# A small DMA for the norm vector, a later parameter packet, and another matmul order in the first chunk

## The chip, the cores and the metric

The kernel runs on one core of a Trainium2 chip. The time is device microseconds (us) of one execution; shown are three runs of the kernel before and, for the profile, one profiled execution. Engines: PE (TensorE, with PEld for its weight loads), DVE (VectorE), ACT (ScalarE), POOL (GpSimd), SP (SyncE, which issues nearly all DMAs). Matmul operands are fp32r: a float32 value is split into a rounded high half and an exact low half.

## The reference

The reference is a trunk of two layers over x of 1 x 256 x 2048 in float32, with RMSNorm ahead of each layer and at the end. Only the beginning matters here:

```python
h = rmsnorm(x, norm_g)                      # x * rsqrt(mean(x*x) + eps) * norm_g
proj = h @ w_in                             # 2048 -> 5120
xa, ga, zb, gb = split(proj)                # zb = (u, v)
ya = s5_mixer(xa, lam_re, lam_im, log_dt, b, c, d)   # constants: exp, cos, sin of lam * dt
...                                         # gates, layernorm of v, spatial gate, w_out, residual
x = x + o @ w_out                           # layer 1: differential attention, rope, w_out
return rmsnorm(x, final_norm)
```

## The kernel before, in words

All weights pass through one stream of chunks, in the order in which they are used: a chunk is 512 rows (four k tiles of 128) by 512 columns, 1 MB. The first eight chunks are the two column blocks of v: chunks 0 to 3 for the first, 4 to 7 for the second. `fetch` (L139) issues a chunk's DMA on SP into a buffer wr; three buffers take turns. Chunks 0 and 1 come in four pieces, 2 and 3 in two, and ahead of each piece comes the piece of x transposed (xt) for the same k tiles. Behind chunk 5 come the two loads of x by tokens (xk), later the other constants.

`split` (L156) makes the halves of a weight: ACT writes wh (rounded), DVE writes wl = w - wh. Both are in half chunks and have three buffers each. `h_split` (L282) does it for the activations, with the norm vector g0 as a scale per partition: ACT writes hh, DVE writes hl. The norm's factor per token is applied to the product later; it comes from `x_norm` (L302): a Square with a running sum on ACT for each xk (scratch tile xsq), then small operations on DVE. `gemm_t` (L201) does three matmuls per k tile and half of the tokens: hh by wh, hh by wl, hl by wh. PE's queue keeps the order of the program, and so do the other engines'.

The parameter packet pkt (L259) holds 164 floats per partition: g0 in columns 0 to 15, then the second norm vector, the parameters of the state space model, biases and others. It is the first DMA. From it `ssm_params` (L359) makes the constants of the state space model with a long run of small DVE operations (`exact_exp`: e_x, e_n, e_r, e_p; then the tiles ph_s, ph_c, pw). `diag_skip` (L452) has POOL write 16 tiles "intra" from it. POOL also fills tiles with zeros (memsets of bbr, cA, cN); cA and cN lie where xk was, so their memsets follow the two xsq.

SP's order is that of the program text. On the other engines a planner sets the order when the kernel is built, with a model of the time of each operation and transfer; work under `high_priority`, as in `split`, `h_split` and `x_norm`, goes ahead of other work that is ready at the same moment. Ten warm-up matmuls on a tile of ones (psw, L269) run before the first weights are there.

Of the kernel before, what the change touches and what calls it, by code (L numbers as in the profile page):

```python
# [10 lines left out]
F32 = mybir.dt.float32  # L11
# [6 lines left out]
T = 256  # L18
# [11 lines left out]
def hybrid_trunk_kernel(ctx: ExitStack, tc: tile.TileContext, xT, xtok, w_in0, w_glu, w_out0,  # L30
# [51 lines left out]
        A.activation(out=o, in_=i, func=f, **kw)  # L82

    def rsqrt_mean(name, ss, n, eps, post=None):
        """(ss / n + eps) ** -0.5: an integer first guess, a cubic step and a Newton step."""
        w = ss.shape[-1]

        def t(nm, dt=F32):
            return sm.tile([128, w], dt, name=nm, tag=f"{nm}{w}", bufs=1)

        def v_y2(y):
            z = t("rq_z")
            if w == 1:
                stt(z, y, v, y, ALU.mult, ALU.mult)
            else:
                mul(z, y, y)
                mul(z, z, v)
            return z

        v = t("rq_v")  # L100
        ts(v, ss, 1.0 / n, ALU.mult, eps, ALU.add)
        g = t("rq_i", I32)
        ts(g, v.bitcast(I32), 1, ALU.logical_shift_right)
        ts(g, g, -1.0, ALU.mult, 1597463007.0, ALU.add)
        y = g.bitcast(F32)
        r = sm.tile([128, w], F32, name=name, tag=name, bufs=2)
        z = v_y2(y)
        u = t("rq_u")
        ts(u, z, 0.375, ALU.mult, -1.25, ALU.add)
        mul(u, u, z)  # L110
        stt(r, u, 1.875, y, ALU.add, ALU.mult)
        z = v_y2(r)
        c = 1.0 if post is None else post
        ts(z, z, -0.5 * c, ALU.mult, 1.5 * c, ALU.add)
        mul(r, r, z)
        return r

    # ---------------------------------------------------------------- weight stream
    stream = []
    L0_IN = {"v": (6, 7), "xa": (0, 1), "u": (4, 5), "gb": (8, 9), "ga": (2, 3)}  # L120
    for part in ("v", "xa", "u", "gb", "ga"):
# [14 lines left out]
    pos = {"f": 0, "s": 0, "i": 0}  # L136
    extra_loads = {}

    def fetch(upto):  # L139
        while pos["f"] <= min(upto, len(stream) - 1):  # L140
            i = pos["f"]
            w, n, k = stream[i]
            t = wp.tile([128, 4, 512], F32, name=f"wr{i}", tag="wr", bufs=3)
            src = w[n, k].rearrange("p (a c) -> p a c", a=4)
            step = (1, 1, 2, 2)[i] if i < 4 else 4
            for a in range(0, 4, step):
                if i < 4:
                    xs = slice(4 * i + a, 4 * i + a + step)
                    SP.dma_start(out=xt[:, xs, :], in_=xT[:, xs, :])
                SP.dma_start(out=t[:, a:a + step], in_=src[:, a:a + step])  # L150
            fetched[i] = t
            for fn in extra_loads.get(i, ()):
                fn()
            pos["f"] += 1

    def split(upto, before=None):  # L156
        """hi = the weight rounded to float32r, lo = the exact rest."""
        while pos["s"] <= min(upto, len(stream) - 1):
            i = pos["s"]
            t = fetched.pop(i)  # L160
            halves[i] = []
            for b in range(2):
                if i >= len(stream) - 4:
                    c = 2 * (i - len(stream) + 4)
                    if b == 0:
                        hb, lb = (t8(LAST[c + z], f"{'hl'[z]}last{i}", [128, 4, 512], F32R) for z in range(2))
                    h, l = hb[:, 2 * b:2 * b + 2], lb[:, 2 * b:2 * b + 2]
                else:
                    h = wp.tile([128, 2, 512], F32R, name=f"wh{i}_{b}", tag="wh", bufs=3)
                    l = wp.tile([128, 2, 512], F32R, name=f"wl{i}_{b}", tag="wl", bufs=3)  # L170
                w = t[:, 2 * b:2 * b + 2]
                with tc.high_priority(offset=AHEAD):
                    step = 1 if i < 2 else 2
                    for a in range(0, 2, step):
                        if before is not None:
                            for z in range(step):
                                before(4 * i + 2 * b + a + z)
                        e = slice(a, a + step)
                        act(h[:, e], w[:, e], AF.Copy)
                        sub(l[:, e], w[:, e], h[:, e].bitcast(F32))  # L180
                halves[i] += [(h[:, a], l[:, a]) for a in range(2)]
            pos["s"] += 1
# [11 lines left out]
    def next_chunk():  # L194
        i = pos["i"]
        pos["i"] += 1
        fetch(i + 3)
        split(i + 1, h_split if i < 3 else None)
        return halves.pop(i)

    def gemm_t(ps, acts, ktiles, first, last):  # L201
        ws = next_chunk()
        for a, k in enumerate(ktiles):
            hi, lo = acts(k)
            wh, wl = ws[a]
            for t in range(2):
                s = slice(t * 128, (t + 1) * 128)
                PE.matmul(ps[:, t, :], hi[:, s], wh, start=first and a == 0, stop=False)  # L208
                PE.matmul(ps[:, t, :], hi[:, s], wl, start=False, stop=False)  # L209
                PE.matmul(ps[:, t, :], lo[:, s], wh, start=False,  # L210
                          stop=last and a == len(ktiles) - 1)

    def gemm_c(ps, acts, ktiles, first, last):
        ws = next_chunk()
# [20 lines left out]
    def side1(name, shape, lane=0):  # L235
        return psb.tile(shape, F32, name=name, tag=f"sb{lane}")

    # ---------------------------------------------------------------- start: x^T, norm
    pkt = const.tile([128, N_PK], F32, name="pkt")
    xt = big.tile([128, 16, T], F32, name="xt", tag="e")  # L240

# [14 lines left out]
    extra_loads[5] = [load_xk]  # L256
    extra_loads[7] = [lambda: SP.dma_start(out=bct, in_=bc)]
    extra_loads[8] = [load_ln]
    SP.dma_start(out=pkt, in_=pk)  # L259
    fetch(8)  # L260
    ident = const.tile([128, 128], F32, name="ident")
    make_identity(nc, ident)
# [4 lines left out]
    psw = side2("psw", [128, 512])  # L267
    for i in range(10):
        PE.matmul(psw[:, 0:128], ones, ones, start=True, stop=True)  # L269
    g0 = pkt[:, 0:16]  # L270
    g1 = pkt[:, 16:32]
    lam_re = pkt[:, 32:64]
    lam_im = pkt[:, 64:96]
# [13 lines left out]

    split(0, h_split)

    # the norm's factor: per token on partitions, and as a row on every partition  # L290
    rbc = const.tile([128, T], F32, name="rbc")
    rsx = {}

# [17 lines left out]
        x_norm()  # L311

    def evac_c(ps, c, name):
        """two of the four channel tiles, times the norm's factor"""
        o = t2(name, [128, 2, T])
        mul(o, ps[:, 2 * c:2 * c + 2, :], rbc.unsqueeze(1).to_broadcast([128, 2, T]))
        return o
# [1 line left out]
    def h_acts(k):  # L319
        return hh[k // 8][:, k % 8, :], hl[k // 8][:, k % 8, :]  # L320

    # ---------------------------------------------------------------- SSM constants
    def p32(name, w=32, dt=F32, bufs=1):
        return sm.tile([128, w], dt, name=name, tag=f"p{w}{name}", bufs=bufs)

# [33 lines left out]
    def ssm_params():  # L359
# [66 lines left out]
        add(fa[:, 1, :], t1, t2_)  # L426
        cst.update(ab=ab, fc=fc, fa=fa, ep=ep)
        yield
        # powers of exp(i * 2 phi): 1, 2, 4, ..., 64
        pw = []  # L430
        prev = ep
        for j in range(7):
# [30 lines left out]
    def ssm_consts():  # L463
# [15 lines left out]
        for key, z_re, z_im, o_re, o_im, sign in (  # L479
# [15 lines left out]
            masked(o_re, m1[:, 0])  # L495
            masked(o_im, m2[:, 0])
            yield
        # K0 = Re(C bb) and the skip, as one matrix per two pairs
        intra = cst["intra"]
        pk0 = side1("pk0", [128, 16, 32])  # L500
        for i in range(16):
# [124 lines left out]
    side.append(e_tables(0))  # L626
    side.append(ssm_consts())

    # ---------------------------------------------------------------- layer 0: v, spatial gate
    G.affine_select(out=bw, in_=bw, pattern=[[0, 8], [1, 128]], compare_op=ALU.is_ge,  # L630
                    fill=0.0, base=0, channel_multiplier=-1)
    vt = t8(13, "vt", [128, 2, 1024])
# [34 lines left out]
    for _ in ssm_bT():  # L667
        pass

    # ---------------------------------------------------------------- layer 0: xa  # L670
    for half in range(2):
        ps = main_c(f"xa{half}")
        for k in range(4):
# [10 lines left out]
        for _ in ssm_half(half):  # L684
            pass

    # ---------------------------------------------------------------- layer 0: u, gb, ga
    ut = t8(8, "ut", [128, 2, 1024])
    for n in range(2):
        ps = main_t(f"u{n}")  # L690
# [44 lines left out]
                gt = evac_c(ps, c, f"at{n}{c}")  # L735
                act(gat[:, n * 4 + 2 * c:n * 4 + 2 * c + 2, :], gt, AF.Silu)

    # ---------------------------------------------------------------- layer 0: output projection
    x1 = [t8(t, f"x1{t}", [128, D]) for t in range(2)]

    def y_acts(k):
# [80 lines left out]
    mul(rope_c, row1, rtab[:, 0])  # L822
    mul(rope_s, row1, rtab[:, 1])

    # ---------------------------------------------------------------- layer 1
    def h2_acts(k):
        return h2h[k // 8][:, k % 8, :], h2l[k // 8][:, k % 8, :]

# [4 lines left out]
    for c in (0, 256):  # L833
        G.affine_select(out=maskt[:, c:c + 128], in_=maskt[:, c:c + 128], pattern=[[-1, 128]],
                        compare_op=ALU.is_ge, fill=NEG, base=0, channel_multiplier=1)
    # lambda
    lprod = const.tile([128, 2], F32, name="lprod")
    lv = lqk.rearrange("p (a b) -> p a b", b=2)
    mul(lprod, lv[:, :, 0], lv[:, :, 1])
# [10 lines left out]
    oh = {}  # L850

    def rope_evac(o, ps, name):
        """o = the rotated, normalised channels; a map's pairs lie on rows 0-15 and 32-47"""
        def row(z, n):
            return z.unsqueeze(1).to_broadcast([n, 4, T])

        m = t4(name, [128, 4, T])
        G.memset(m[0:32], 0.0)
        mul(m[0:16], ps[32:48], row(rope_s[32:48], 16))
        mul(m[32:48], ps[0:16], row(rope_s[0:16], 16))  # L860
        mul(o, ps, row(rope_c, 128))
        add(o[0:48], o[0:48], m[0:48])
# [78 lines left out]
    for p in range(4):  # L941
        qk_hl = []
        for w in range(2):
# [2 lines left out]
                gemm_c(ps, h2_acts, range(k * 4, k * 4 + 4), k == 0, k == 3)  # L946
                run_side(1)
            rope_evac(qkT[:, w], ps, f"rm{p}{w}")
            # the second query block meets all keys: its operands in two exact parts
            src = qkT[:, w, :, 128 * (1 - w):T]  # L950
            hi, lo = (z[:, 512 * w:512 * w + 512 * (1 + w)].rearrange("p (m t) -> p m t", m=4) for z in (qk_hi, qk_lo))
            act(hi, src, AF.Copy)
# [16 lines left out]
        side.append(attention(p, qkT, qk_hl, vh, vl, sg))  # L969
        run_side(1000)  # L970

    # ---------------------------------------------------------------- layer 1: output projection
    def o_acts(k):
        a, b = oh[k // 8]
        return a[:, k % 8, :], b[:, k % 8, :]
# [63 lines left out]
def _layout(i):  # L1039
# [11 lines left out]
    xT = np.ascontiguousarray(x.T.reshape(16, 128, T).transpose(1, 0, 2))  # L1051
    xtok = np.ascontiguousarray(x.reshape(2, 128, D))

    # pairs of groups, ordered (half, qh, ct, q) where the pair is half * 16 + ct * 4 + qh * 2 + q
    order = np.arange(32).reshape(2, 4, 2, 2).transpose(0, 2, 1, 3).reshape(32)

    def state(z):
# [31 lines left out]
    rp[0:16, 0] = rp[32:48, 0] = c  # L1089
    rp[0:16, 1] = z  # L1090
    rp[32:48, 1] = -z
    # rows 16-31 and 32-47 of every map of q and k change places
    d = np.arange(128)
    d[16:32], d[32:48] = np.arange(32, 48), np.arange(16, 32)
    cols = np.concatenate([(np.arange(32)[:, None] * 128 + d).reshape(-1), np.arange(4096, 8192)])
# [29 lines left out]
```

## Time and profile before

| | us |
|---|---|
| median of 3 runs | 888.91 |
| lowest, highest | 888.35, 889.16 |
| span of the profiled execution, first to last instruction | 887.3 |
| PE busy | 871.7 (98%) |
| DVE busy | 666.3 (75%) |
| ACT busy | 448.8 (51%) |
| POOL busy | 38.3 (4%) |
| DMA | 160.24 MB, mean 181 GB/s |

The page gives for the profiled execution its span alone; the runs are timed apart and contain what lies around the span. Times in the rows count from the first instruction. Busy time of PE overlaps from one matmul to the next, so the pace of PE is read from start to start. The column of the granted clock reads 1.00 throughout the beginning; that the first matmuls run at half pace is seen only from their starts.

### The profile page before, as it was taken

To read this page: it belongs to the slowest core of one execution; us is meant where nothing else is said; L and a number is where in the kernel's file an instruction comes from. 1 tells how busy PE (TensorE), PEld (TensorE's weight loads), DVE (VectorE), ACT (ScalarE), POOL (GpSimd) and SP (SyncE) were. 2 spreads that over 40 slices of the span, in tenths; PEclk is the share of its full clock that TensorE was granted. 3 is DMA by queue.
4 is the path that set the end of the run, shared out by engine and by line. 5 is a ranking of instruction groups with operands and counts; after the bars stand their busy time and mean duration, and the time that the engine had idled before them with its cause. 6 is when DMAs were issued, how large, how long until landed. Compare 5 with 4: busy or idle time off the path is not lost.

```text
span 887.3 us, 14016 instructions
## 1 busy us (share of the span) xinstructions
PE 871.7 (98%) x5598; PEld 778.4 (88%) x5598; DVE 666.3 (75%) x1219; ACT 448.8 (51%) x623; POOL 38.3 (4%) x47
## 2 busy tenths in 40 slices
PE   9999999999999999999999999999999999999995
PEld 7799978788999789889988999889988998888895
DVE  8999869999988866567866677666767577665773
ACT  6563862455334645565345543554346544554551
POOL 7110000000000100000000000000000000000000
PEclk9999999999999999999999999999999999999998
DMA  8965452234534655455554545554454455555542
GB/s 306 379 243 191 143 190 96 96 120 166 190 114 141 259 185 176 170 195 202 180 182 160 188 145 190 191 190 152 181 190 171 165 188 196 183 189 190 178 155 96
DMA packets 25985, 160.24 MB, mean 181 GB/s; under 512 B 2880, under 2 KB 4160, under 8 KB 7744
## 3 DMA queue, kind: packets, MB, share of 16 engines
q1 hardware_dynamic: 25344, 156.20, 49.2%
q0 software_dynamic: 576, 3.15, 1.0%
q8 instruction: 44, 0.72, 0.3%
q14 instruction: 21, 0.17, 0.1%
HBM read 157.24 MB, written 2.10 MB: 180 GB/s over the span
## 4 chain that ended last, share of the span: by engine, by line
PE 90%; DVE 7%; ACT 1%; issue 1%; DMA 0%; DVEq 0%; ACTq 0%
PE v L209 5%; PE v L210 5%; PE v L208 5%; PE k L224 3%; PE q L221 3%; PE k L223 3%; PE k L221 3%; PE q L224 3%; PE q L223 3%; PE g L210 3%; PE g L209 3%; PE g L208 3%; PE od L209 2%; PE od L208 2%; PE od L210 2%; PE ga L221 2%
## 5 line engine op out<-in xcount | busy, mean ns | idle before, releaser
L82 ACT ACTIVATE wh<-wr 128x1024 fp32r<-128x1024 f32 (+1 forms) x276 | 288.7, 1047 | 356.0 <-PE v L210 64.0
L61 DVE TENSOR_TENSOR wl<-wr,wh 128x1024 fp32r<-128x1024 f32 (+1 forms) x276 | 331.8, 1205 | 142.2 <-ACT wh L82 141.4
L224 PE MATMUL k<-h2h,wl 128*128 128x256 f32 x256 | 72.8, 284 | 0.0
L221 PE MATMUL q<-h2h,wh 128*128 128x256 f32 x256 | 72.7, 284 | 0.0
L223 PE MATMUL q<-h2l,wh 128*128 128x256 f32 x256 | 72.7, 284 | 0.0
L224 PE MATMUL q<-h2h,wl 128*128 128x256 f32 x256 | 72.6, 284 | 0.0
L221 PE MATMUL k<-h2h,wh 128*128 128x256 f32 x256 | 72.4, 283 | 0.0
L223 PE MATMUL k<-h2l,wh 128*128 128x256 f32 x256 | 72.4, 283 | 0.0
L209 PE MATMUL v<-wl,h2h 128*128 128x512 f32 x128 | 50.8, 397 | 0.0
L209 PE MATMUL g<-wl,h2h 128*128 128x512 f32 x128 | 50.3, 393 | 0.0
L210 PE MATMUL g<-wh,h2l 128*128 128x512 f32 x128 | 50.1, 391 | 0.0
L210 PE MATMUL v<-wh,h2l 128*128 128x512 f32 x128 | 50.0, 390 | 0.0
L208 PE MATMUL v<-wh,h2h 128*128 128x512 f32 x128 | 50.0, 390 | 0.0
L208 PE MATMUL g<-wh,h2h 128*128 128x512 f32 x128 | 49.9, 390 | 0.0
L224 PEld LDWEIGHTS k<-h2h,wl 128*128 128x128 f32 x256 | 49.1, 192 | 0.1
L221 PEld LDWEIGHTS q<-h2h,wh 128*128 128x128 f32 x256 | 49.1, 192 | 0.2
L221 PEld LDWEIGHTS k<-h2h,wh 128*128 128x128 f32 x256 | 49.1, 192 | 0.0
L223 PEld LDWEIGHTS k<-h2l,wh 128*128 128x128 f32 x256 | 49.1, 192 | 0.0
L223 PEld LDWEIGHTS q<-h2l,wh 128*128 128x128 f32 x256 | 49.1, 192 | 0.0
L224 PEld LDWEIGHTS q<-h2h,wl 128*128 128x128 f32 x256 | 49.1, 192 | 0.0
L209 PE MATMUL od<-wl,oh 128*128 128x512 f32 x96 | 37.6, 392 | 0.0
L208 PE MATMUL od<-wh,oh 128*128 128x512 f32 x96 | 37.5, 391 | 0.0
(331 smaller groups left out, 2182.8 us busy)
## 6 DMA issues: line engine op xcount, KB each, us to landing
wr<-in_w_in_dram SPq DMA_DIRECT2D x100, 1024.0 KB, 4.8
wr<-in_w_out_dram SPq DMA_DIRECT2D x32, 1024.0 KB, 4.8
wr<-in_w_glu_dram SPq DMA_DIRECT2D x4, 1024.0 KB, 4.7
wr<-in_w_in_dram SPq DMA_DIRECT2D x8, 256.0 KB, 4.5
wr<-in_w_in_dram SPq DMA_DIRECT2D x4, 512.0 KB, 7.9
xk<-in_xtok_dram SPq DMA_DIRECT2D x2, 1024.0 KB, 10.9
xr<-in_xtok_dram POOLq DMA_DIRECT2D x2, 1024.0 KB, 7.6
out_dram<-x SPq DMA_DIRECT2D x6, 256.0 KB, 2.6
```

The costliest lines, as they stand in the source:

```text
L61: (eng or V).tensor_tensor(out=o, in0=a, in1=b, op=op)
L82: A.activation(out=o, in_=i, func=f, **kw)
L208: PE.matmul(ps[:, t, :], hi[:, s], wh, start=first and a == 0, stop=False)
L209: PE.matmul(ps[:, t, :], hi[:, s], wl, start=False, stop=False)
L210: PE.matmul(ps[:, t, :], lo[:, s], wh, start=False, stop=last and a == len(ktiles) - 1)
L221: PE.matmul(ps[:, c, :], wh[:, s], hi, start=first and a == 0 and c % 2 == 0, stop=False, skip_group_check=True)
L223: PE.matmul(ps[:, c, :], wh[:, s], lo, start=False, stop=False, skip_group_check=True)
L224: PE.matmul(ps[:, c, :], wl[:, s], hi, start=False, stop=fin, skip_group_check=True)
```

## The change

The diff also blanks comment lines. What it does to the program:

- g0 gets a tile of its own, loaded by the first DMA from columns 0 to 15 of the packet (64 B per partition).
- The DMA of the whole packet is issued behind the second piece of chunk 0's weights.
- In chunk 0 the six matmuls of a k tile come in another order: hh by wh for both token halves, hl by wh for both, hh by wl for both. In all other chunks the order stays: hh by wh, hh by wl, hl by wh, for one half and then the other.

```diff
@@ fetch
                 SP.dma_start(out=t[:, a:a + step], in_=src[:, a:a + step])
+                if i == 0 and a == 1:
+                    SP.dma_start(out=pkt, in_=pk)
@@ gemm_t
+        low_last = pos["i"] == 0
         ws = next_chunk()
         for a, k in enumerate(ktiles):
             hi, lo = acts(k)
             wh, wl = ws[a]
-            for t in range(2):
-                s = slice(t * 128, (t + 1) * 128)
-                PE.matmul(ps[:, t, :], hi[:, s], wh, start=first and a == 0, stop=False)
-                PE.matmul(ps[:, t, :], hi[:, s], wl, start=False, stop=False)
-                PE.matmul(ps[:, t, :], lo[:, s], wh, start=False,
-                          stop=last and a == len(ktiles) - 1)
+            ops = [(t, x, w) for t in range(2) for x, w in ((hi, wh), (hi, wl), (lo, wh))]
+            if low_last:
+                ops = ops[0::3] + ops[2::3] + ops[1::3]
+            for j, (t, x, w) in enumerate(ops):
+                PE.matmul(ps[:, t, :], x[:, t * 128:(t + 1) * 128], w, start=first and a == 0 and x is hi and w is wh,
+                          stop=last and a == len(ktiles) - 1 and (x is lo if not low_last else w is wl))
@@ start
-    SP.dma_start(out=pkt, in_=pk)
+    g0 = const.tile([128, 16], F32, name="g0")
+    SP.dma_start(out=g0, in_=pk[:, 0:16])
     fetch(8)
...
-    g0 = pkt[:, 0:16]
```

## Rows read from the trace of the kernel before

**Rows 1.** The page, first line: span and instructions.
```profile
span 887.3 us, 14016 instructions
```

**Rows 2.** Stages: window, its length, busy us of each engine (instructions), PEclk, DMA share, GB/s.
```profile
5.00:10.00 5.00, 4.10 (x11) 2.81 (x11) 4.90 (x20) 3.92 (x8) 5.00 (x7) 1.00 0.97 320
...
20.00:32.00 12.00, 12.00 (x55) 9.94 (x54) 11.38 (x49) 7.19 (x11) 0.00 (x0) 1.00 1.01 408
...
60.00:110.00 50.00, 50.00 (x500) 48.53 (x499) 47.29 (x91) 29.55 (x39) 0.00 (x0) 1.00 0.48 169
```

**Rows 3.** Waits of PE: who waited for whom; total us, times, longest.
```profile
PE v L209 <- DVE wl L61: 1.6, 2, 0.8
PE gb L208 <- ACT ut L82: 1.4, 1, 1.4
```

**Rows 4.** Timeline of PE: start us, us, operation, [idle before, releaser].
```profile
5.85 0.80 PE L208 MATMUL v<-wh,hh 128*128 128x512 f32 x1
7.47 0.80 PE L209 MATMUL v<-wl,hh 128*128 128x512 f32 x1 [0.82 <-DVE wl L61]
...
9.77 0.63 PE L208 MATMUL v<-wh,hh 128*128 128x512 f32 x1
10.20 0.53 PE L209 MATMUL v<-wl,hh 128*128 128x512 f32 x1
...
19.89 0.39 PE L209 MATMUL v<-wl,hh 128*128 128x512 f32 x1
...
42.64 0.50 PE L209 MATMUL v<-wl,hh 128*128 128x512 f32 x1 [0.83 <-DVE wl L61]
```

**Rows 5.** Timeline of DVE, 0 to 20 us.
```profile
2.70 1.88 DVE L76 TENSOR_SCALAR e_x<-pkt 128x32 f32<-128x32 f32 x1 [1.62 <-DMA pkt<-in_pk_dram]
...
6.36 0.17 DVE L74 TENSOR_SCALAR e_n<-e_n 128x32 f32<-128x32 f32 x1
...
6.74 0.68 DVE L61 TENSOR_TENSOR wl<-wr,wh 128x512 fp32r<-128x512 f32 x1
...
18.31 1.22 DVE L61 TENSOR_TENSOR wl<-wr,wh 128x1024 fp32r<-128x1024 f32 x1 [0.27 <-ACT wh L82]
```

**Rows 6.** Timeline of ACT, 5 to 39 us.
```profile
5.17 0.63 ACT L82 ACTIVATE wh<-wr 128x512 fp32r<-128x512 f32 x1 [1.13 <-DMA wr<-in_w_in_dram]
...
17.22 1.06 ACT L82 ACTIVATE wh<-wr 128x1024 fp32r<-128x1024 f32 x1 [0.86 <-PE v L210]
...
31.95 1.92 ACT L82 ACTIVATE xsq<-xk 128x2048 f32<-128x2048 f32 x1
...
37.01 1.06 ACT L82 ACTIVATE wh<-wr 128x1024 fp32r<-128x1024 f32 x1 [0.21 <-DVE pw L61]
```

**Rows 7.** Timeline of DVE, 34 to 42 us.
```profile
34.67 1.19 DVE L74 TENSOR_SCALAR ph_c<-ph_c 128x32 f32<-128x32 f32 x1
...
38.14 0.56 DVE L76 TENSOR_SCALAR pw_m<-pw_m 128x32 f32<-128x32 f32 x1
...
41.38 1.21 DVE L61 TENSOR_TENSOR wl<-wr,wh 128x1024 fp32r<-128x1024 f32 x1
```

**Rows 8.** Timeline of POOL, 34 to 39 us.
```profile
34.01 1.81 POOL L469 MEMSET cA<- 128x2048 f32 x1 [16.01 <-ACT xsq L82]
36.85 1.81 POOL L470 MEMSET cN<- 128x2048 f32 x1 [1.03 <-ACT xsq L82]
```

**Rows 9.** Issues at 1.26, 3.15, 10.58 and 22.04 us: KB, us to landing.
```profile
xt<-in_xT_dram SPq DMA_DIRECT2D x1, 128.0 KB, 2.2
xt<-in_xT_dram SPq DMA_DIRECT2D x1, 128.0 KB, 4.3
wr<-in_w_in_dram SPq DMA_DIRECT2D x1, 512.0 KB, 6.5
xk<-in_xtok_dram SPq DMA_DIRECT2D x1, 1024.0 KB, 9.9
```

**Rows 10.** DMA queues, 2.0 to 2.3 us: packets, MB, share of 16 engines.
```profile
q1 hardware_dynamic: 104, 0.06, 65.8%
```

## The prediction

> **What bounds the kernel now.** I read the page, then the table by stages, the waits of PE, and last the timelines of the first 45 us. The reader is to see that PE fills its stage where nothing disturbs it, 50.00 of 50 us from 60 to 110 [rows 2], so that a microsecond taken from PE's early waits counts only if PE brings it that far. PE's list of waits [rows 3] has two for a low half wl in "v", 1.6 us together: one ends at 7.47 us, one at 42.64 us [rows 4]. The change goes for the first; the second tells whether a gain lasts.
>
> The first: PE runs one matmul at 5.85 us, as soon as wh of k tile 0 is there, and stands until 7.47 us for wl of that tile. DVE began this wl only at 6.74 us, though wh was finished at 5.17 + 0.63 = 5.80: the small operations of the SSM constants were ahead of it in its queue, and the first of them, e_x, had taken 1.88 us for 32 elements, where such an operation takes 0.17 [rows 5, 6].
>
> The second: PE has done the first matmul of chunk 6 and is idle for 0.83 us until that chunk's wl is there, at 42.64 us [rows 4]. This wl began on DVE at 41.38 us, though its wh was done at 37.01 + 1.06 = 38.07 [rows 6, 7]: it stood behind small operations in DVE's order. DVE is without a gap in that stretch, but two operations in it are waits in disguise: TENSOR_SCALARs of 1.19 us at 34.67 and of 0.56 us at 38.14. They end at 35.86 and 38.70, just after POOL's memsets of cA (34.01 + 1.81 = 35.82) and cN (36.85 + 1.81 = 38.66) [rows 7, 8]. The memset of cA had waited for the first xsq on ACT, which starts at 31.95 us, and that is when xk lands: issued at 22.04, 9.9 us on its way [rows 6, 9]. So PE's restart at 42.64 hangs on a DMA that lands at 31.94 us, with 10.7 us of ACT, POOL and DVE work between, and PE's own pace is not in it. The chain of waits goes from 42.64 back to a matmul at 30.7 us; it takes the 1.19 us at 34.67 for DVE's work.
>
> **The change part by part.**
>
> *Order of matmuls in chunk 0.* The count stays 24. Ahead of the first wl there are now four matmuls in place of one. At the early pace, 0.43 us from one to the next (512 columns at 1.2 GHz), they last until 5.85 + 4 x 0.43 = 7.57 us [rows 4]. wl of the old order was done at 6.74 + 0.68 = 7.42 [rows 5], so this wait goes even if DVE does nothing sooner. The second matmul comes at 6.28 in place of 7.47: 1.19 us. From 10.20 to 19.89 us there are 42 matmuls, 0.23 us each, that is 2.4 GHz [rows 4]. If the pace doubles at 10.4 us as now, 1.19 / 0.43 = 2.8 more matmuls are done by then, worth 2.8 x 0.23 = 0.6 us. If it doubles sooner, as PE now works without a break from 1.1 us on, the gain grows, to at most 1.19 + (10.4 - 6.3) / 2 = 3.2 us. I take 0.6, the way the rows have it; it will not matter which.
>
> *Where this gain ends.* PE uses wl of k tile 8 (the 50th matmul) at 19.89 us; DVE finishes it at 18.31 + 1.22 = 19.53 [rows 4, 5]. It can hardly be sooner: wh of that tile began at 17.22, and its weights, issued at 10.58 us, land 6.5 us later, at 17.08 [rows 6, 9]. So PE can be ahead by 19.89 - 19.53 = 0.36 us there at most, less what the stream of DMAs loses.
>
> *The packet behind two pieces.* Now its 82 KB come first, when the DMA engines have nothing else, and cost nothing. xt's first piece lands at 1.26 + 2.2 = 3.46 us [rows 9]. I take it that this and the first wr land as before; if they came sooner by the time that the packet leaves free, this too would be spent at k tile 8. In the new place the packet's data come behind the second wr, and from 5 to 32 us the engines are 97 to 101% busy [rows 2]: everything behind moves by the packet's share. 104 of its packets took 65.8% of 16 engines during 0.3 us [rows 10], 30 ns of an engine each; 128 packets over 16 engines are 0.24 us. Ends: 0, if it finds gaps, and 0.36, if its engines were taken whole while it ran (0.3 x 128 / 104). I take 0.24, the row's own. SP's one more issue is hidden: what it issues at 3.15 us lands 4.3 us later [rows 9], so SP is far ahead of the engines.
>
> *The norm vector.* 128 packets of 64 B where 128 of 656 B went; no row has one so small. Ends: 0 and the 0.36 us of the packet. Either way it is through before xt's data come, and the first hh is unmoved.
>
> By the Trainium skill, DMA: Bandwidth & Descriptors, section Specifications, pieces under 512 B are read, modified and written back. No row here shows this; if it made the vector twice as long as the packet was, xt and the stream behind it would be some 0.4 us later and the sum by as much above mine.
>
> *DVE.* e_x cannot start before the packet lands, at 3.15 + 4.3 = 7.4 us or a little sooner [rows 9], in place of 2.70. hl and wl of k tile 0 no longer stand behind it: wl can run at 5.80, 0.94 us sooner. The eleven small operations that DVE did before 7.4 us come later, at most 11 x 0.17 = 1.9 us [rows 5]. What covers this lag is that DVE stands still for POOL at 34.67 and 38.14, (1.19 - 0.17) + (0.56 - 0.17) = 1.4 us [rows 7]: with 1.9 - 0.94 = 1.0 us of lag it arrives later and waits less. If the cover were gone, the 1.0 us would be PE's.
>
> *POOL.* The 16 intra operations need the packet too and start 2 to 3 us later; nothing reads their result in this stretch, and the memset of cA waits for ACT.
>
> **The sum.** PE gains 0.6 us at the start; at k tile 8, 0.36 - 0.24 = 0.12 are left; before 42 us it waits again for chunk 6's wl, now 0.12 longer. That wl follows the landing of xk, 0.24 us later than now. PE restarts at 42.64 + 0.24 and is the bound from there: the span is 887.3 + 0.24 = 887.54 us [rows 1]. The median of the timed runs lies 888.91 - 887.3 = 1.6 us above the profiled span, which I take for what lies around it: 889.15 us. That is no change by 0.2% (1.78 us), about what a measurement of this kernel can tell.
>
> **The rivals.**
>
> *The second wait goes too.* DVE's order is written by a planner that sees the packet come later; it may set chunk 6's wl ahead of some ten small operations that precede it now. At 0.1 us each (they overlap) that is 1.0 us sooner, enough for the 0.83. For it: wh was ready 3.3 us before its wl began. Against: the planner places a wl by when it expects its wh, and that hardly moves. PE then keeps its 0.12 as well: 887.3 - 0.95 = 886.35, 887.95 us.
>
> *Slower: DVE's lag gets past the memsets.* Place: DVE from 34.67 to 42.6 us. If the small operations stay ahead of chunk 6's wl and lag by more than the 1.4 us of standing for POOL, each further microsecond is one of PE. e_x ended at 2.70 + 1.88 = 4.58 and would end at 7.6, a lag of 3.0 us; less the 0.94 that wl gains, 2.1. Then 2.1 - 1.4 + 0.24 = 0.9 longer, 888.2, 889.85 us; without the 0.94 it is 890.8. Against it: most of what DVE did before 4.58 us was standing.
>
> *The first wait stays,* because e_x is ahead of the first wl in DVE's queue and waits there for the packet. wl would be done at 7.4 + 0.2 + 0.7 = 8.3, and PE would wait 0.7 us after four matmuls, and its fifth now comes at about 7.47 + 3 x 0.43 = 8.8, so it is ahead still: the sum is the forecast's.
>
> *The waits further on are dealt anew.* Behind 110 us PE has four waits, of 1.4 us at the longest [rows 3]. A planner with other times may add or take 2 us there: 887.1 or 891.1.
>
> **How the numbers follow.** Forecast, with the first wait gone or not, 889.15: 0.42. Second wait gone, 887.95: 0.30. DVE's lag, 889.85 to 890.8: 0.16. Dealt anew: 0.12, half each way. The range 887.4 to 890.4 holds the first, nearly all of the second and most of the third, and leaves out the fourth: some 0.2. Below 888.91 - 1.78 = 887.13 lie half of the fourth and a little of the second: 0.09. Above 890.69 lie its other half and a little of the third: 0.08. Within: 0.83.
>
> **What would show it.** First step: PE's second matmul at 6.3 us and no wait of PE before 10 us. DVE: e_x at 7 us or later, of 0.2 us. The gain spent: wl of k tile 8 done at 19.5 to 19.9, with PE waiting for it. Stream and anchor: xsq at 32.2, PE's restart at 42.9. I am wrong if PE passes chunk 6 without a wait, if xsq moves by more than 0.5 us, or if the two kernels part in a stage behind 60 us.

## The result: slower by half a per cent, lost around 105 to 120 us

The changed kernel takes 893.79 us (median of 4 runs, 893.31 to 895.89); the ratio to the kernel before is 1.0055, 95% interval 1.0043 to 1.0068, some 4.9 us. The forecast of no change was wrong. The first line of its page, and two stages of [rows 2] with three more windows, read:

```profile
span 892.1 us, 14018 instructions
```
```profile
5.00:10.00 5.00, 4.39 (x18) 3.16 (x18) 3.07 (x9) 3.20 (x6) 2.87 (x5) 1.00 0.91 292
...
60.00:110.00 50.00, 47.81 (x490) 46.35 (x489) 48.65 (x94) 27.07 (x34) 0.00 (x0) 1.00 0.48 171
110.00:220.00 110.00, 105.11 (x618) 87.11 (x617) 92.00 (x184) 54.01 (x67) 0.00 (x0) 0.98 0.35 125
...
118.00:120.00 2.00, 0.41 (x1) 0.41 (x2) 2.00 (x3) 0.84 (x1) 0.00 (x0) 0.77 0.00 0
120.00:122.00 2.00, 2.00 (x6) 1.52 (x6) 2.00 (x3) 1.08 (x2) 0.00 (x0) 0.50 0.69 197
```

From 5 to 10 us PE runs 18 matmuls in place of 11, and DVE is busy for 3.07 us in place of 4.90. From 60 to 110 us PE, which had filled that stage [rows 2], stands for 2.2 us; from 110 to 220 us it is busy for 105.11 us, where it was 106.60. PE's waits, summed over the whole span, were 6.62 us and are 11.30: 4.7 us more. That this is near the 4.8 us by which the span grew is in part chance, since PE also lost time at a lower clock (below) and got some back later. The list of PE's waits of the changed kernel, longest groups first, has waits of "u" of 1.3 to 2.1 us; in the kernel before, "u" waited once for wl (0.8 us) and once for ut (0.5 us):

```profile
PE u L214 <- DVE wl L61: 2.1, 1, 2.1
PE v L214 <- DVE wl L61: 1.8, 3, 0.8
PE u L214 <- ACT wh L82: 1.4, 1, 1.4
PE u L214 <- DVE rq_i L74: 1.3, 1, 1.3
...
PE pbt L525 <- DVE intra L61: 0.8, 1, 0.8
```

Its timeline of PE (the first six lines answer to [rows 4]):

```profile
5.89 0.96 PE L214 MATMUL v<-wh,hh 128*128 128x512 f32 x2
6.69 0.63 PE L214 MATMUL v<-wh,hl 128*128 128x512 f32 x2
7.16 0.63 PE L214 MATMUL v<-wl,hh 128*128 128x512 f32 x2
...
19.39 0.50 PE L214 MATMUL v<-wh,hh 128*128 128x512 f32 x1 [0.64 <-ACT wh L82]
20.65 0.50 PE L214 MATMUL v<-wl,hh 128*128 128x512 f32 x1 [0.76 <-DVE wl L61]
...
43.52 0.50 PE L214 MATMUL v<-wl,hh 128*128 128x512 f32 x1 [0.80 <-DVE wl L61]
...
104.18 0.28 PE L228 MATMUL xa<-hh,wl 128*128 128x256 f32 x1
105.26 0.63 PE L525 MATMUL pbt<-ident,bbr 128*128 128x128 f32 x4 [0.80 <-DVE intra L61]
107.15 0.50 PE L214 MATMUL u<-wh,hh 128*128 128x512 f32 x1 [1.26 <-DVE rq_i L74]
...
117.00 0.50 PE L214 MATMUL u<-wh,hh 128*128 128x512 f32 x1 [1.40 <-ACT wh L82]
119.59 0.80 PE L214 MATMUL u<-wl,hh 128*128 128x512 f32 x1 [2.08 <-DVE wl L61]
120.18 0.63 PE L214 MATMUL u<-wh,hl 128*128 128x512 f32 x1
120.61 0.63 PE L214 MATMUL u<-wh,hh 128*128 128x512 f32 x1
```

The kernel before had at this place:

```profile
102.92 0.28 PE L224 MATMUL xa<-hh,wl 128*128 128x256 f32 x1
...
103.40 0.48 PE L208 MATMUL u<-wh,hh 128*128 128x512 f32 x1
```

At 43.52 us PE is 0.88 us behind the kernel before, at the last matmul of "xa" 1.26 us (102.92 before). Four waits then cost 5.5 us between 105 and 120 us, where the kernel before had three between 113 and 135 us, of 0.77, 0.76 and 0.46.

The waits are not all. Between 115.21 and 119.59 us PE starts one matmul only, and in that stretch the granted clock falls from 1.00 to 0.50. Seven matmuls from 119.59 us on start 0.43 us apart, the pace of 1.2 GHz, and take 3.03 us; the seven behind the wait at 113.06 us in the kernel before take 1.72. That is 1.3 us more. The kernel before has a granted clock of 1.00 from 100 to 140 us.

The wait at 107.15 is the one to read. The profile names rq_i as its releaser, an operation of one element that "u" does not read. On DVE it is simply what follows xs, the evacuation of xa0, and "u" needs xs: with two accumulators for xa0, xa1 and u0, u0 gets the one that xs empties. DVE of the changed kernel, and DVE of the kernel before, at this place:

```profile
102.33 0.69 DVE L61 TENSOR_TENSOR m1ab<-m1ab 128x512 f32<-128x512 f32 x1
...
103.73 1.38 DVE L61 TENSOR_TENSOR intra<-pk,intra 32x512 f32<-32x512 f32 x2
105.14 0.69 DVE L79 SCALAR_TENSOR_TENSOR m2ab<-m2ab 128x512 f32<-128x512 f32 x1
105.87 1.22 DVE L61 TENSOR_TENSOR xs<-xa,rbc 128x1024 f32<-128x1024 f32 x1
107.01 0.14 DVE L74 TENSOR_SCALAR rq_i<-rq_v 128x1 int32<-128x1 int32 x1
```
```profile
98.32 0.68 DVE L61 TENSOR_TENSOR m1ab<-m1ab 128x512 f32<-128x512 f32 x1
...
101.72 1.22 DVE L61 TENSOR_TENSOR xs<-xa,rbc 128x1024 f32<-128x1024 f32 x1
102.86 0.14 DVE L74 TENSOR_SCALAR rq_i<-rq_v 128x1 int32<-128x1 int32 x1
```

PE finished xa0, the first half of the 384 matmuls of "xa", near 77 us in the kernel before and near 78 us in the changed one. Its xs runs more than 20 us later, at the very end of the SSM constants (m1ab, m2ab), in both kernels. Before, xs ended at 102.94 and PE came to "u" at 103.40: 0.46 us to spare, and no wait to show it. Now xs ends at 107.09 and PE starts "u" at 107.15. Behind xs, ACT has eight copies of it to make before the next wh, and the planner has also put both vt ahead of that wh, where before it had wh first:

```profile
108.30 5.30 ACT L82 ACTIVATE U<-xs 32x512 f32<-32x512 f32 x8
113.62 2.38 ACT L82 ACTIVATE vt<-vt,vnb,vrs 128x1024 f32<-128x1024 f32 x2
115.91 2.94 ACT L82 ACTIVATE wh<-wr 128x1024 fp32r<-128x1024 f32 x3
```
```profile
105.36 5.30 ACT L82 ACTIVATE U<-xs 32x512 f32<-32x512 f32 x8
110.68 1.06 ACT L82 ACTIVATE wh<-wr 128x1024 fp32r<-128x1024 f32 x1
111.65 1.23 ACT L82 ACTIVATE vt<-vt,vnb,vrs 128x1024 f32<-128x1024 f32 x1
```

The first of these three wh begins 5.2 us later than the wh at 110.68: 2.9 us because the copies start later, 2.3 us because of the two vt. It releases the matmul at 117.00, and its wl (118.31 on DVE, behind three vt operations) the one at 119.59.

### The profile page after: what moved, and what is told of

Its sections match the earlier page's. It is cut to its first block, busy times and chain, and to the rows that moved or that the text cites. A ratio compares the mean times of both kernels' runs of the same rounds, so it can differ in the third digit from the quotient of the medians.

```text
span 892.1 us, 14018 instructions
## 1 busy us (share of the span) xinstructions
PE 871.4 (98%) x5598; PEld 777.8 (87%) x5598; DVE 665.4 (75%) x1219; ACT 449.3 (50%) x623; POOL 34.6 (4%) x47
## 3 DMA queue, kind: packets, MB, share of 16 engines
q0 software_dynamic: 576, 3.15, 1.0%
## 4 chain that ended last, share of the span: by engine, by line
PE 90%; DVE 5%; ACT 2%; DMA 1%; issue 1%; SPq 1%; DVEq 0%; ACTq 0%
PE v L214 10%; PE g L214 10%; PE od L214 7%; PE gb L214 5%; PE eo L214 5%; PE ep L214 5%; PE u L214 4%; PE k L228 3%; PE q L225 3%; PE k L227 3%; PE k L225 3%; PE q L228 3%; PE q L227 3%; PE W L572 2%; PE y L610 2%; PE ga L227 2%
```

## The experiments

The table has what is needed of each: the ratio to the kernel before on the same chip with its 95% interval, and from one profile when DVE ended e_x and began xs, in us.

| kernel | median us | ratio [95%] | e_x ends | xs begins |
|---|---|---|---|---|
| before | 888.74 | | 4.58 | 101.72 |
| after | 893.79 | 1.0055 [1.0043, 1.0068] | 7.16 | 105.87 |
| order_only | 889.39 | 0.9999 [0.9990, 1.0008] | 4.58 | 101.03 |
| late_only | 893.54 | 1.0045 [1.0033, 1.0058] | 7.18 | 105.87 |
| stream_only | 890.10 | 1.0006 [0.9997, 1.0016] | 4.58 | 101.39 |
| chain_mid | 889.40 | 1.0001 [0.9992, 1.0010] | 5.18 | 100.69 |
| chain_late | 893.96 | 1.0050 [1.0036, 1.0063] | 8.42 | 105.67 |
| chain_later | 895.54 | 1.0066 [1.0053, 1.0079] | 10.50 | 107.32 |
| logdt_early | 890.09 | 1.0010 [1.0001, 1.0019] | 2.84 | 102.82 |
| after_less | 889.04 | 0.9996 [0.9987, 1.0004] | 6.98 | 98.48 |
| before_less | 886.50 | 0.9968 [0.9956, 0.9979] | 4.58 | 96.31 |
| memsets_split | 889.54 | 1.0000 [0.9991, 1.0009] | 5.46 | 102.96 |
| unlocked | 889.56 | 1.0002 [0.9994, 1.0011] | 3.08 | 101.62 |
| unlocked_order | 889.65 | 1.0005 [0.9995, 1.0014] | 3.14 | 101.70 |
| after_own_xs | 887.99 | 0.9986 [0.9978, 0.9995] | 7.42 | 79.78 |
| before_own_xs | 888.06 | 0.9983 [0.9974, 0.9991] | 4.54 | 78.78 |
| order_own_xs | 887.75 | 0.9980 [0.9971, 0.9988] | 4.54 | 78.33 |
| chain_later_own_xs | 889.82 | 1.0002 [0.9994, 1.0011] | 10.41 | 81.08 |

**Which part costs.** order_only is the kernel before with the new gemm_t alone; late_only is the changed kernel with the old one.

> The kernel before with only the matmul order of chunk 0 changed; all DMAs as before. Theory (DVE start: the changed kernel loses 4.8 us because DVE's chain of SSM constants starts 4.3 us later, DVE has no free time until 105 us, and PE pays between 103 and 120 us): the chain starts at 2.7 us as before, so the time is that of before within 1 us, 888.7 (887.9 to 889.2), and PE's waits between 103 and 135 us are those of before, 2.0 us. Rival 1 (the new matmul order gives the planner other times and it deals the later waits anew): 892 or more. Rival 2 (the packet's data in the busy DMA stream): as before, 888.7.

> The changed kernel with the matmul order of before: the norm vector alone in front and the packet behind two pieces. Theory (DVE start): nothing is won back, 893.8 (892.8 to 894.6), e_x at about 7 us, the layernorm's rq_v at 103 to 104 us as in the changed kernel (99.5 before). Rival 1 (matmul order and planner): 888.7. Rival 2 (stream): 893.8 too.

The order is free and gains nothing; the late packet is all of the loss that can be told from the spread of the runs. late_only has the same waits at 105.26, 107.14, 116.98 and 119.56 us (0.80, 1.26, 1.34, 2.09) as the changed kernel.

**The packet's place in the stream, or what reads it.** stream_only is the kernel before with a second, unread load of the packet behind the second weight piece; chain_late reads one field, log_dt, from a DMA of its own at that place, and leaves the packet first; logdt_early is the changed kernel with log_dt beside the norm vector in the first DMA. The edit of chain_late:

```diff
+                if i == 0 and a == 1:
+                    SP.dma_start(out=ldt, in_=pk[:, 96:128])
...
-    log_dt = pkt[:, 96:128]
+    log_dt = ldt
```

> The kernel before with a second load of the whole packet behind the second piece of weights, into a tile that nobody reads; the packet itself first as before, the old matmul order. It is one more DMA in the stream and nothing waits for it. Theory (one more DMA among those in flight, whatever its size, delays the stream by more than its bytes): xsq and k tile 8 come 0.6 to 1.0 us later, and the time is 0.5 to 1.0 us above before. Rival (bytes alone): 0.24 us. The theory of the DVE start says that none of the 4.8 us comes from here.

> The kernel before with the packet first as before and the old matmul order; but log_dt, with which the chain of SSM constants starts, is read from a second small DMA (16 KB) behind the second piece of weights. The DMA stream is the old one but for 16 KB. Theory (DVE start): the late start alone costs it all: 893.5 (892.5 to 894.5). Rival 1 (matmul order): 888.7. Rival 2 (82 KB in the stream): at most 0.1 us, 888.8.

> The changed kernel with one difference: log_dt is beside the norm vector in the first DMA (48 columns, 24 KB); the packet stays behind two pieces and the new matmul order stays. Theory (DVE start): e_x runs at 2.7 to 4.6 us as before, and the loss goes: 888.9 (888.2 to 890). Rival 1 (matmul order) and rival 2 (82 KB in the stream): it stays, 893.8.

chain_late loses as much as the changed kernel with 16 KB moved; logdt_early gets back all but 0.1%, a little less than expected (890.09 us, at most 890 expected). So nearly all of the loss comes through e_x, the head of the chain of SSM constants on DVE. stream_only is undecided: its interval reaches from 0.3 us faster to 1.4 us slower and holds both expectations.

**The dose.** chain_mid and chain_later are chain_late with the DMA behind the first and the fourth piece.

> As chain_late, but the small DMA of log_dt is behind the first piece of weights: e_x ends at about 6 us, 1.4 us later than before (chain_late: 8.4, 4.6 us slower; chain_later: 10.5, 6 us slower). The planner's order of ACT is that of before. Theory (each microsecond of DVE's lag is one of PE once the cover is used): 0.5 to 1.8 us slower than before. Rival (cover of 1.4 us by the stands for POOL, as predicted): 0.3 us or less.

> As chain_late, but the small DMA of log_dt is behind the fourth piece of weights, so that e_x starts at about 10 us, 2 to 3 us later than in chain_late. Theory (DVE volume): DVE is idle for longer, and the time grows by a part of that, 1 to 2.5 us above chain_late, 895 to 896.5. Rival (planner's order): DVE's order behind 60 us is nearly that of chain_late, so the time is within 0.7 us of it, 893.3 to 894.7.

e_x later by 0.6 us costs nothing, by 2.6 and 3.8 some 4 to 5 us, by 5.9 about 5.9: a threshold first, then a jump. chain_mid came out as its rival said, but with e_x only 0.6 us late and not 1.4 it is a weak test. The landing of xk differs from profile to profile, so the lag is seen better when xs is counted from the start of the first xsq: 69.7 to 70.0 us in before, order_only, stream_only, chain_mid and logdt_early, 73.1 to 73.3 in after, late_only and chain_late, 75.1 in chain_later. An e_x that is 2.6 us late thus makes xs 3.5 us late, more than its own lag. In chain_mid ACT's order behind 100 us is still that of before, in the two others it is that of the changed kernel. This and the two vt ahead of a wh point to the planner's other order as a part of the loss. No run has a late e_x under the order of before, so how large that part is stays open.

**Less work on DVE.** after_less and before_less leave out half of the last doubling of the first table E (zeros stand there).

```diff
+        if half == 0:
+            G.memset(E[:, :, 8:16, 64:128], 0.0)
...
-            for q in range(2):
+            for q in range(1 if half == 0 and k == 6 else 2):
```

> The changed kernel without the last doubling of the second quarter of the first table of exponentials (eight operations on DVE of 128x512, 4 us, at 60 to 90 us; zeros are there instead). Theory (DVE volume: DVE has no free time from 5 to 105 us, so 4 us less of its work give back what its late start took): 3 to 4.5 us faster than the changed kernel, 889.3 to 890.8. Rival (what was lost is the planner's other order of ACT and DVE at 103 to 120 us): within 1.5 us of the changed kernel, 892.3 or more.

> The kernel before without the last doubling of the second quarter of the first table of exponentials (4 us of DVE, zeros in its place), the cut of after_less. Theory (in the kernel before DVE is just not late: PE waits only 2.0 us at 110 to 135 us for it): it gains 0 to 1.5 us, much less than the 4.5 us that the same cut gave the changed kernel. Rival (the cut gives any kernel 4 us): 885.

What goes is six operations of DVE, not eight as the first text has it. With it xs begins 7.4 us sooner in the changed kernel (6.5 us counted from xsq), and its four waits at 105 to 120 us are gone; 2.8 us come off the kernel before as well, where at most 1.5 were expected. Two readings were left by this: DVE is short of time as a whole, or one thing at the end of its chain is late.

**A DVE that stands less.** memsets_split cuts POOL's long memsets in eight pieces each; unlocked writes the steps of exp() as SCALAR_TENSOR_TENSOR with constants in a tile, which did not stand for POOL; unlocked_order adds the new matmul order.

```diff
-            G.memset(bbr[c], 0.0)
+            for j in range(8):
+                G.memset(bbr[c][:, 4 * j:4 * j + 4], 0.0)
...
```
```diff
-        ts(n, xc, 1.4426950408889634, ALU.mult)
-        ts(n, n, MAGIC, ALU.add)
...
+        stt(n, xc, 1.4426950408889634, fix[:, 1, 0:w], ALU.mult, ALU.add)
...
```

> The kernel before with POOL's four memsets of zeros (bbr twice, cA, cN) cut into eight pieces each; everything else, the order on PE, DVE and ACT too, is the same. An operation of DVE that stands for POOL then waits for a piece of some 0.25 us and not for the whole. Theory (DVE time early in the kernel is PE's time): e_x ends at about 3.2 in place of 4.6 us, the two operations at 34.67 and 38.14 are short, chunk 6's wl comes 1 us sooner and PE's wait of 0.83 us at 42 goes: 0.7 to 1.8 us faster than before. Rival (a late chain costs by the planner's order alone, DVE's own times are covered): the same within 0.3 us. Rival (cutting does not help, since DVE waits for the run of pieces): the same.

> The kernel before with the clamping and rounding steps of the chain's exponential written as operations with two tensor inputs (three constant tiles of 128x32), so that they do not stand for POOL's memset at 2.7 to 4.5 us; five DVE operations fewer per exponential. Theory (DVE time at the start is PE's time): the chain is 1.9 us ahead at 4.6 us, PE's wait of 0.83 us at 42 shrinks or goes and the next at 113 to 136 us shrink: 0.7 to 2 us faster than before. Rival (a late chain costs, an early one gains nothing, since PE's restart at 42 hangs on xk's landing and the memsets that follow it): the same within 0.4 us.

> As unlocked, with the changed kernel's matmul order in chunk 0 as well. Theory: PE's first wait goes too; it gains what PE can carry past k tile 8, 0 to 0.5 us beyond unlocked. Rival: as unlocked.

In all three the theory misses and the rival of no gain comes out. memsets_split did not get e_x sooner at all (the last section has it). In unlocked e_x 1.5 us sooner buys nothing, and xs begins where it did: a part of the lead is spent where DVE stands for POOL's memset of cN, 1.70 us at 37.22 in place of 0.56. A lead of DVE is worth nothing, a lag of 2.6 us is PE's; where between 0.6 and 2.6 us that begins was not run.

**The dependency itself.** xs is taken from the ring "t4" of three buffers that the temporaries of the SSM constants use too, and the scratch tiles vscr of v's layernorm. The profile does not name the buffers, but the times of ACT in the changed kernel fit one reading:

```profile
101.07 1.27 ACT L82 ACTIVATE bbr<-m2fa 64x512 f32<-64x512 f32 x2
102.38 1.15 ACT L82 ACTIVATE vscr<-vt,mu 128x1024 f32<-128x1024 f32 x1
...
104.71 0.19 ACT L82 ACTIVATION_READ_ACCUMULATOR vscr<-vt,mu 128x1 f32 x1
...
105.75 1.25 ACT L82 ACTIVATE cA<-m1ab 64x512 f32<-64x512 f32 x2
```

m1ab and m2ab still hold two buffers when xs starts at 105.87, since ACT reads them until 107.00 and 108.29. The third goes from m2fa (read until 102.34) through the two vscr (until 104.90) to xs, which then stands behind intra and m2ab in DVE's order. By this reading xs does not wait for the buffers of m1ab and m2ab, as the texts below have it, but for the temporaries ahead of them and for its place in DVE's order. Four kernels give xs0 the buffer of the scan's state, which is free until then.

```diff
-    ya = {}
-    hst = sm.tile([128, 2, 4, 129], F32, name="hst", tag="hst")
-    G.memset(hst[:, :, :, 0:1], 0.0)
+    ya, hst = {}, []
...
+        if not hst:
+            hst.append(sm.tile([128, 2, 4, 129], F32, name="hst", tag="hst"))
+            G.memset(hst[0][:, :, :, 0:1], 0.0)
...
-            xs = t4(f"xs{half}", [128, 4, T])
+            xs = t4("xs1", [128, 4, T]) if half else sm.tile([128, 4, T], F32, name="xs0", tag="hst")
```

> The changed kernel, but the evacuation of xa0 (xs0) writes the buffer of the scan's state (free until then) and not the t4 ring, where it had to queue behind the products m1ab and m2ab of the SSM constants; xs0 then stands some 23 places earlier in DVE's order. Theory A (the loss is handed to PE through this ring: SSM constants late, so xs0 late, so u0's accumulator late, so U2's copies and the next wh late): PE's wait at 107.15 us (1.26) is gone, the two behind it (1.40 and 2.08) shrink below 1 together, total 888.5 to 890.5 us. Theory B (DVE as a whole has too little time before 120 us, whatever its order): the waits on wl at 117 to 120 us stay or grow, total 892.5 to 895 us.

> The kernel before with the same other buffer for xs0. Theory A: there xs0 ended about 0.5 us before PE asked for the buffer, so nothing was lost and nothing is gained: 887.8 to 889.3 us. Theory B: xs0 put ahead of the SSM constants makes these about 1.1 us later on a full DVE: 889 to 891 us.

> The kernel before with the other matmul order of the first chunk and the other buffer for xs0; packet where it was. Theory A: as the order alone, 888 to 889.5 us, the lead of the start spent at k tile 8. If the 0.77 us wait at 113 us goes with the ring, some 0.5 us less. Theory B: 889 to 891 us.

> The kernel with log_dt from a DMA behind the fourth weight piece (895.54 us, DVE's chain 5.8 us behind that of before), with the other buffer for xs0. Theory A: most of its 6.6 us come back, 889 to 891.5 us. Theory B: 894 to 897 us, since DVE's lag is as large as before.

Theory A of these four texts holds in its waits, and more came back than it said: after_own_xs is below its range, and before_own_xs, where nothing was to be gained, is 0.17% faster. With the packet late as in the change, the waits around 107 and 117 us are gone from the list of PE's waits of after_own_xs:

```profile
PE v L214 <- DVE wl L61: 1.9, 3, 0.8
PE v L214 <- ACT wh L82: 1.4, 2, 0.7
...
PE u L214 <- ACT ut L82: 0.5, 1, 0.5
PE pbt L525 <- ACT bT L82: 0.3, 1, 0.3
```

Its DVE runs xs in the middle of table E, and ends the SSM constants later than the changed kernel did (m1ab at 103.72 against 102.33 us):

```profile
79.78 1.22 DVE L61 TENSOR_TENSOR xs<-xa,rbc 128x1024 f32<-128x1024 f32 x1
...
103.72 0.68 DVE L61 TENSOR_TENSOR m1ab<-m1ab 128x512 f32<-128x512 f32 x1
```

So the constants may be late, and DVE as full as before; what cost PE was that xs stood behind them. Theory B is out for the loss of the change. It is not the whole of the kernel before: there some 4 us less of DVE's work took off 2.8 us, the other buffer 1.5 us, and the two together were not run. The other buffer brings 0.69% back with the late packet (1.0055 to 0.9986), 0.64% in chain_later, and 0.17% in the kernel before, whose 0.77 us wait for wl at 113 us is gone with it. Beside before_own_xs, the late packet then costs nothing that can be measured (0.9986 against 0.9983). chain_later_own_xs keeps some 0.2%: there the lag shows earlier, as waits of 1.40 and 0.77 us for wl at 40.7 and 44.5 us. The granted clock, which falls to 0.50 between 105 and 125 us in the profiles of the four kernels that lose (after, late_only, chain_late, chain_later), stays at 1.00 between 25 and 875 us in those of all the others. The other buffer lets the planner lay out 75 to 135 us anew, so the runs show that xs's place in the ring is the cause, not how much of the gain each moved operation has. The three versions at 0.9980 to 0.9986 beat both kernels and can't be told apart.

## Why the prediction was wrong, step by step

*Order of matmuls, the gain at the start: right, and larger than taken.* Twelve matmuls run from 5.89 us in one go, the wait at 7.47 is gone. From 6.69 us on they start 0.23 us apart, so the pace doubled sooner than the 10.4 us that I took, and behind chunk 0 PE is 1.7 us ahead (12.54 against 14.23) where I took 0.6; my upper end was 3.2. "No wait of PE before 10 us" was not quite so: 0.49 us at 9.64 for a wh, as that weight came later.

*Where this gain ends: right in the place.* PE waits at 19.39 and 20.65 us for wh and wl of k tile 8, and order_only alone is worth 0.0%. With the later stream nothing of it was left: PE is 0.76 us behind there (20.65 against 19.89), not 0.12 ahead.

*The packet in the stream: too small, and not settled.* wh of k tile 8 began 1.06 us later (18.28; [rows 6] have 17.22), and xsq at 32.62 in place of 31.95, 0.67 us where I took 0.24. But in stream_only's profile, with the same bytes in the same place, xsq began at 31.41, and in order_only and memsets_split, with the DMAs of before, at 31.27 and 34.08: two profiles differ by more than the term. The norm vector's small pieces showed nothing at the start: the first wh began at 5.21 us against 5.17, and in the four profiles with the vector in front at 5.14 to 5.29, within the 4.74 to 5.49 of the others. By the Trainium skill, DMA: Bandwidth & Descriptors, section Specifications, transfers below 512 B are read, modified and written. The 0.4 us that I had estimated for that did not appear at this place.

*DVE, what comes sooner and later: right in its numbers.* wl ran at 5.87 (5.80 said), e_x at 6.98 for 0.18 us (7.4 "or a little sooner").

*"What covers this lag": the step that failed.* I set the lag (1.0 us) against DVE's standing for POOL at 34.67 and 38.14 [rows 7], 1.4 us that would shrink. It did not shrink: the memset of cA had moved too, with xsq (34.66 + 1.83 = 36.49), and met other operations of the chain. The second standing is gone and the first is longer, 1.65 - 0.17 = 1.5 us in all. DVE of the changed kernel, then pw_sq of the kernel before:

```profile
34.88 1.65 DVE L76 TENSOR_SCALAR e_i<-e_n 128x32 int32<-128x32 f32 x1
35.00 1.55 DVE L74 TENSOR_SCALAR ph_s<-ph_z 128x32 f32<-128x32 f32 x1
...
40.50 0.22 DVE L61 TENSOR_TENSOR pw_sq<-ep 128x64 f32<-128x64 f32 x1
...
42.24 1.22 DVE L61 TENSOR_TENSOR wl<-wr,wh 128x1024 fp32r<-128x1024 f32 x1
```
```profile
36.26 0.22 DVE L61 TENSOR_TENSOR pw_sq<-ep 128x64 f32<-128x64 f32 x1
```

Above all I looked for the lag in the wrong operations. The wl that PE waits for is only 0.86 us later (41.38 in [rows 7]), because weights go ahead of the constants in DVE's order; the same stretch has pw_sq 4.2 us later than before. A full DVE hands its lag to the work of least priority, and that work then kept it: m1fc began at 84.68 in place of 80.67 and m1ab ended 4.0 us later. PE, which reads nothing of it for 50 us, has no wait in its list from 44 to 105 us and shows nothing.

*"PE … is the bound from there": failed for the same reason.* It held to the last matmul of "xa" (PE 1.26 us behind). Then the end of the constants had a hold on PE that no wait of the profile before shows, since xs was 0.46 us early there: the ring "t4". The size follows, roughly: xs later by 4.15 us (0.67 of it from the later xsq), less those 0.46 and less PE's own 1.26, leaves 2.4 us, of which the waits at 105.26 and 107.15 are 2.06. More came behind it: 3.48 us of waits for wh and wl at 117 and 119.59 in place of 1.99 us (0.77, 0.76, 0.46), and 1.3 us of matmuls at half pace, which the prediction did not have. At the last matmul of "u" PE is 5.7 us behind (175.91 against 170.25), at its last matmul of all 4.4 (882.42 against 878.03); how it got the difference back was not followed up.

*The rivals.* "DVE's lag gets past the memsets" was right in kind, at 889.85 to 890.8 too cheap, and put at 34.67 to 42.6 us where only 0.88 us of the loss is found. "The waits further on are dealt anew" had the place (behind 110 us, where the list has five waits and not four) and, in the two vt ahead of a wh, some of the manner, but left the sign to chance; it was not chance: the four kernels with e_x at 7 us or later, all work and the shared ring (after, late_only, chain_late, chain_later) lose 0.45 to 0.66%, and the two of these that got a buffer for xs0 lose nothing against the kernel before that can be measured. "The two kernels part in a stage behind 60 us" was a sign that I had named for being wrong, and it is what happened; xsq moved by more than the 0.5 us of another such sign, but it does so between profiles with the same DMAs too.

## What to carry to other kernels

A lag on a full engine shows up in the work of least priority, so follow that work to its end and ask what shares a buffer ring, an accumulator or a queue with it there; a bound engine that is busy all along says nothing of a release that is half a microsecond early. Two long waits close together can cost more than their length: here the clock fell as well. When a wait's named releaser is something the waiter does not read, look at the operation that ran just before it on that engine. And where a ring ties urgent work to slack work, try a buffer of its own for the urgent work: here it gave 0.17% without a lag and 0.69% with one.

## What was not expected of the hardware

In memsets_split POOL's memsets of bbr are sixteen pieces of about 0.26 us, the last fourteen of them in one run, and e_x on DVE still stood until the run was over, 2.67 us, longer than for the unbroken memsets (1.88 us [rows 5]); the second operation that began beside it stood too. DVE and POOL of that kernel:

```profile
2.79 2.67 DVE L76 TENSOR_SCALAR e_x<-pkt 128x32 f32<-128x32 f32 x1 [1.71 <-DMA pkt<-in_pk_dram]
2.88 2.58 DVE L61 TENSOR_TENSOR lprod<-pkt 128x2 f32<-128x2 f32 x1
5.49 0.32 DVE L74 TENSOR_SCALAR e_n<-e_x 128x32 f32<-128x32 f32 x1
```
```profile
1.83 3.60 POOL L467 MEMSET bbr<- 128x256 f32 x14
```

DVE goes on at 5.46 us, where the memsets end at 5.43. Cutting POOL's work in pieces did not let DVE in between them; that the same steps as SCALAR_TENSOR_TENSOR (unlocked, e_x ended at 3.08 us) did not stand is what helped there. Why is open: no run here shows it.
